# Attention scores as alternating 64-row matmuls in a hybrid attention and mLSTM kernel on one NeuronCore

## The chip, the core and the metric

The kernel runs on one core of one Trainium2 chip. The metric is the device time of one execution in microseconds (us), lower is better. Before the change three runs gave 1333.98, 1334.25 and 1334.64 us; their median, 1334.25 us, is the time before.

## The reference, cut to what matters

Two layers (DEPTH 2) work on 512 tokens of width 1024 in float32. Each layer projects the normalised input once and runs two branches from it: differential attention with 8 heads and an mLSTM with 8 heads. Both are gated, projected back and added. The change is in the attention branch alone. Each head has two maps `r` with their own queries and keys of 64 elements, and one value of 128:

```python
q = rope(rmsnorm(two_map_heads(aq), q_norm_g), cos, sin)   # (1, 8 heads, 512, 2 maps, 64)
k = rope(rmsnorm(two_map_heads(ak), k_norm_g), cos, sin)
...
sc = jnp.einsum('bhqrd,bhkrd->bhrqk', qb, k).astype(jnp.float32) * scale   # qb: a block of 128 queries
p = jax.nn.softmax(jnp.where(causal, sc, -jnp.inf), axis=-1)
a = p[:, :, 0] - lam * p[:, :, 1]
return jnp.einsum('bhqk,bhkd->bhqd', a.astype(v.dtype), v)
```

The sum over `d` in the first einsum runs over 64 elements, half of the 128 rows of TensorE.

## The kernel before, in words

**Precision.** TensorE takes its operands as `float32r` tiles. To keep float32 accuracy every operand is split into a part `hi` that ACT casts and a rest `lo` that DVE subtracts (`split`, line 489), and a product is the sum of three matmuls, hi by hi, hi by lo and lo by hi (`mm3`, line 493).

**Pieces.** A layer is a list of pieces, one for each 128 x 1024 block of weights (`qk0` to `qk3` are the projections of query and key, `av`, `bv` the values, `az`, `ga`, `gb`, `bo`, `bz` the gates, `bqk` the mLSTM's query and key, `woa`, `wob`, `wo` the output projections). `TUNE["order"]` gives their order. Each piece is a run of 128-row matmuls over 512 columns, and between the pieces the steps of the attention heads (`attn_head`, line 1166) and mLSTM heads (`ml_head`) become due at times counted in steps of the pieces (`TUNE["attn"]`, `a0`, `ap`, `ml`, `m0` and so on).

**Order on the engines.** All operations are recorded first (`Recorder.add`, line 165, with a planned cost from `cost`, line 218), then a list scheduler (`schedule`, line 272) simulates five engines and emits one order for each. Its keys are the due times, the costs, a bias for each tile name (`TUNE["bias"]`) and several margins. The order that it emits is fixed in the program; on the chip every engine takes its own list in order and waits for semaphores.

**Scores before.** One piece group `qk c` holds heads 2c and 2c+1. `qk_done` (line 832) takes the tiles and applies norm and rotation; `back` in `qk_back` (line 897) transposes the 128 tokens by 512 features on TensorE into the PSUM tile `qkt` and evicts them to SBUF. There the 64 features of map 0 lie in partitions 0 to 63 and those of map 1 in 64 to 127. The eviction builds for each map a stacked query tile `[hi; lo]` of 128 rows (`qs0`, `qs1`), a key tile `[hi; hi]` (`ks0`, `ks1`), and a key rest `kl0`, `kl1` whose other 64 rows POOL sets to zero (`half_zero`, line 617). For even `c` the first four are parts of a large tile `qk..x`; for odd `c` they are tiles of a pool of 20 slots (`take`, `give`). Then a score needs two matmuls of 128 rows for each map: `[hi; lo]` by `[hi; hi]`, and `[hi; lo]` by `[lo; 0]`. In `qk(j)` (line 1170) `j` counts the four blocks of 128 queries, and n = 128 (j+1) columns of keys are computed, so n is 128, 256, 384 and 512. With two layers, eight heads and four blocks there are 64 such steps of four matmuls each, 256 in all, 64 of each n. The two maps are in two PSUM banks of one tile `sc`.

**Other 8- and 128-row work that the prediction uses.** `gft` and `gct` are transposes of gate rows with only 8 rows in use (four matmuls each, twice in a program); `glf` are transposes with 128 rows and only 8 columns. `msp_a` is the sum over partitions for the norm of an attention head: two matmuls with a matrix of ones (`msh_a`, `msl_a`), or one where a head is in `TUNE["foldA"]` (`ms_front`, line 1276): there DVE adds the two halves first (`fo_a`).

Of the kernel before, what the change touches and what calls it, by code (L numbers as in the profile page):

```python
# [9 lines left out]
F32 = mybir.dt.float32  # L10
# [25 lines left out]

TUNE = {
    "order": (
# [4 lines left out]
    ),  # L43
    "qkt": 5,
    "gct": 15,
    "gls": 6,
    "glf": 5,
    "attn": (1, 5, 5, 8, 9, 13, 15, 16, 19, 24),
    "a0": 23,
    "ap": 18,  # L50
    "a4": 7,
    "ml": (1, 9, 11, 12, 13, 28),
    "ahead": 3,
    "lc": 7,
    "slack": 4956.0,
    "margin": 72.0,
    "pemargin": 206.2,
    "wait": 333.1,
    "swpen": 141896579.9,
    "smargin": 51.6,  # L60
    "pwait": 0.7,
    "wdiff": 3673.3,
    "wsp": 4,
    "kact": (0, 2),
    "qsq": (1, 3),
    "foldA": (2, 3, 5),
# [4 lines left out]
    "prods": 'P1 P5 P2 P6 P3 P7 P4',  # L71
    "acl": 14,
    "gateA": 9,
    "gateM": 4,
    "actp": (0, 2, 3),
    "m0": 217,
    "mp": 15,
    "m4": 9,
    "slots": 20,
    "bias": {'av': 30400.0, 'msp_a': -4350.0, 'wl': 2200.0, 'wo': -3700.0, 'woh': -4650.0, 'ht': 29250.0, 'taz': -4050.0, 'ga': 25150.0, 'gt': -8800.0, 'p': -900.0, 'wo1_P': 27550.0, 'out_0_dram': -5850.0, 'p5_wo': -4950.0, 'rot': 12400.0, 'dq': -4400.0, 'oa': 450.0, 'dd': 31000.0, 'num': 20100.0, 'ld': -7300.0, 'ws1_wo': -2200.0, 'gw': -1100.0, 'hl': -600.0, 'sc': -1500.0, 'uz': -3750.0, 'mk': 7950.0, 'sbz': 4200.0, 'az': 12900.0, 'posi': 3200.0, 'msl_d': 1650.0, 's1_wo': 5000.0, 'msh_d': 6450.0, 'sq': -1400.0, 'warm': 3150.0, 'bo': -450.0, 'sdl': 150.0, 'ml': 16100.0, 'fo_b': 12850.0, 'ws0_wo': -900.0, 'wt1_wo': 1400.0, 'pb': 8800.0, 'sbo': 5350.0, 'qkt': 3900.0, 'junk': 7400.0, 'ulZ': 6400.0, 'bv': 650.0, 'bqk': -1750.0, 'uh': -3950.0, 'ms_b': -1100.0, 'ob': -400.0, 'uy': 1500.0, 'ms': 11100.0, 'ms_a': 1750.0, 'ones': 4150.0, 'msh_b': 8300.0, 'x1d': -3000.0, 'saz': 1000.0, 'xr': -3950.0, 'wo0_P': 450.0, 'qk1_0x': 2050.0, 'msh_a': 6050.0, 'rnh': -3150.0, 'gft': 6600.0, 'gct': 3100.0, 'kl': -700.0, 'qk1_2x': -800.0, 'gf': 1550.0, 'qk0_0x': -1600.0, 'qy': 7250.0, 'msl_a': 1400.0, 'x': -4550.0, 'eps': -600.0, 'wt0_wo': -2500.0, 'xn': 400.0, 'msl_b': 2150.0, 'rn': -400.0, 'glf': -3500.0, 'ss': 7600.0, 'sinv': 6150.0, 'ulA': -2650.0, 'epsc': -3000.0, 'ulB': 950.0, 'ulY': -300.0, 'tbz': 350.0, 'hh': 3700.0, 'fo_a': 6500.0, 'mx': -1800.0, 'gc': -150.0, 'mq': -1050.0, 'ang': 3150.0, 'qt': -2500.0, 'uhZ': -1250.0, 'em': -6800.0, 'ct': 1000.0, 'fo_d': 3850.0, 'par': -250.0, 'ks': 250.0, 'den': -400.0, 'sdh': -1000.0, 'cv': -300.0, 'ng': 3750.0, 'uhB': 300.0, 'rows': -300.0, 'zw': 50.0, 'qs': 1350.0, 'ctab': 950.0, 'gcol': 3400.0, 'ul': 1000.0, 'fb_b': 400.0, 'sums': 400.0, 'cosv': 250.0},  # L80
    "drain": 467.1,
    "risk": 268.4,
    "late": 912.7,
}


# [16 lines left out]
class Recorder:  # L103
# [113 lines left out]
    @staticmethod  # L217
    def cost(eng, fn, a, k):
        def cols(ap):
            n = 1  # L220
            for x in list(ap.shape)[1:]:
                n *= x
            return n

        def ps(ap):
            return isinstance(ap, bass.AP) and ap.space == PSUM

        n = cols(a[0])
        if eng == "PE" and a[0].tensor.name.startswith("warm"):
            return 350.0  # L230
        if eng == "PE":
            n = cols(a[2]) if fn == "matmul" else cols(a[0])
            return max(n / 2.4 + 13.4, 107.5)
        if eng == "POOL":
            return 1000.0 if fn == "dma_start" else 200.0 + n
        if eng == "ACT":
            x = 52 + n * 0.833 + (0 if ps(a[1]) else 42)
            for v in (k.get("bias"), k.get("scale")):
                if isinstance(v, bass.AP):
                    x += 93  # L240
            if k.get("accum_out") is not None:
                x += 93
            return x
        if eng == "DVE":
            aps = [v for v in a[1:] if isinstance(v, bass.AP)]
            if fn == "reciprocal":
                return 64 + 6.26 * n
            if fn == "memset":
                return 8 + n * 1.04
            if fn == "tensor_reduce":  # L250
                return 69 + cols(a[1]) / 0.96
            if fn == "tensor_tensor_scan":
# [192 lines left out]
def kernel(ctx, tc, x, pos, wp, wg, cst, par, pb, ngb, out):  # L445
# [180 lines left out]
    def layer_events(l):  # L626
# [204 lines left out]

        def qk_done(c, tt, acc):
            if tt == 0:
                names = ("qs0", "qs1", "ks0", "ks1")
                if c % 2 == 0:
                    until(lambda: c == 0 or st.get(("A", 1), 0) > 5)
                    xt = big.tile([P, 8, S], F32R, tag="big", name=f"qk{l}_{c}x")
                    st[("qs", c)] = [xt[:, 2 * i : 2 * i + 2, :] for i in range(4)]
                    take(2)
                else:  # L840
                    take(6)
                    st[("qs", c)] = [q2(f"{n}{l}_{c}") for n in names]
                st[("kl", c)] = [half_zero(f"kl{r}{l}_{c}", r) for r in range(2)]
                st[("rq", c)] = cp.tile([P, NT, 8], F32, tag=f"rq{c % 2}", name=f"rq{l}_{c}")
            sq = t2(f"sq{l}_{c}_{tt}")
            if tt % 2 == 0:
# [41 lines left out]
        def qk_back(c, tt, rq):  # L888
            k3 = rq[:, 256:512].rearrange("p (g d) -> p g d", d=64)
            rk = st[("rq", c)][:, tt, 4:8].unsqueeze(2).to_broadcast([P, 4, 64])  # L890
            if tt in TUNE["kact"]:
                for g in range(4):
                    A.activation(k3[:, g, :], k3[:, g, :], AF.Copy, scale=st[("rq", c)][:, tt, 4 + g : 5 + g])
            else:
                V.tensor_tensor(k3, k3, rk, ALU.mult)

            def back():
                pst = ps_tr.tile([P, 4, P], F32, tag="tr", name=f"qkt{l}_{c}_{tt}")
                for g in range(4):
# [12 lines left out]

            defer(TUNE["qkt"], back)
# [252 lines left out]
        def attn_head(h, t0):  # L1166
# [3 lines left out]
            def qk(j):  # L1170
                n = P * (j + 1)
                sc = ps_sc.tile([P, 2, S], F32, tag="sc", name=f"sc{l}_{h}_{j}")
                qs = slice(j * P, (j + 1) * P)
                q, k, kl = st[("qs", c)][0:2], st[("qs", c)][2:4], st[("kl", c)]

                for r in range(2):
                    T.matmul(sc[:, r, :n], q[r][:, hl, qs], k[r][:, hl, :n], start=True, stop=False)
                    T.matmul(sc[:, r, :n], q[r][:, hl, qs], kl[r][:, hl, :n], start=False, stop=True)
                if j == 3 and hl:
                    give(2 if c % 2 == 0 else 6)  # L1180
                dg = sc[:, :, n - P : n]
                V.tensor_tensor(dg, dg, mask_a.unsqueeze(1).to_broadcast([P, 2, P]), ALU.add)
                mx = small(2, f"mx{l}_{h}_{j}")
# [462 lines left out]
```

## Time and profile before

| what | value |
|---|---|
| median of three runs | 1334.25 us (1333.98 to 1334.64) |
| profiled execution, first to last instruction (span) | 1333.4 us |
| granted TensorE clock | 0.999 |
| PE / PEld busy | 99% / 82%, 6200 instructions each |
| DVE / ACT / POOL busy | 76% / 68% / 3% |

The page gives no other time of the profiled execution than its span; the median of the runs lies 0.85 us above it. PE is TensorE's matmul queue and PEld its weight loads (LDWEIGHTS), of which every matmul has one. A matmul's printed duration runs from its start to its modelled end and overlaps its successor, so what a matmul costs in a stream is read from the distance between starts: in the stream of 512-column matmuls that is 0.23 us, though each is printed with 0.39. Rows of a timeline read: start, time taken by the row, engine, line, operation, out<-in, rows*columns of the array in use, shape, and how many were merged.

### The profile page before, as it was taken

How to read it: one execution, taken by the hardware profiler on the slowest of the kernel's cores; microseconds unless marked ns; L12 is line 12 of the kernel's file. 1: busy time of each engine (PE TensorE's matmuls, PEld its weight loads, DVE VectorE, ACT ScalarE, POOL GpSimd, SP SyncE). 2: the span in 40 equal slices, each digit the busy share in tenths (PEclk: the TensorE clock that was granted, in tenths of full speed). 3: DMA queues.
4: the chain of work that ended last, by engine and by line, in shares of the span. 5: the costliest groups of instructions: out<-in, count | busy, mean ns of one | idle time of the engine just before them, and what ended most of it. 6: DMA issues, size and time to landing. Idle time of an engine off the chain costs nothing.

```text
span 1333.4 us, 17564 instructions
## 1 busy us (share of the span) xinstructions
PE 1326.1 (99%) x6200; PEld 1096.4 (82%) x6200; DVE 1018.1 (76%) x1846; ACT 907.4 (68%) x1836; POOL 37.0 (3%) x44
## 2 busy tenths in 40 slices
PE   8999999999999999999999999999999999999998
PEld 7888888888888888888888888888888888888887
DVE  7898899786259967755888988997852698687466
ACT  5878888877237958743667787888762478687243
POOL 1000000000000000000200000000000000000000
PEclk9999999999999999999999999999999999999999
DMA  5222222323344433544832121223232444345546
GB/s 188 87 65 79 80 80 64 95 79 94 100 121 124 119 114 109 154 148 123 258 125 88 49 96 54 89 67 92 82 110 81 123 134 124 98 129 148 170 123 181
DMA packets 51274, 148.15 MB, mean 111 GB/s; under 512 B 6097, under 2 KB 12881, under 8 KB 51185
## 3 DMA queue, kind: packets, MB, share of 16 engines
q1 hardware_dynamic: 48880, 138.63, 33.5%
q0 software_dynamic: 2304, 8.39, 3.5%
q8 instruction: 49, 0.80, 0.3%
q14 instruction: 41, 0.33, 0.1%
HBM read 142.74 MB, written 4.26 MB: 110 GB/s over the span
## 4 chain that ended last, share of the span: by engine, by line
PE 97%; ACT 1%; DVE 1%; DMA 0%; issue 0%; SPq 0%; DVEq 0%
PE qk L441 13%; PE av L441 9%; PE az L441 7%; PE bv L441 7%; PE bo L441 7%; PE bqk L441 7%; PE ga L441 7%; PE woa L441 7%; PE wob L441 7%; PE gb L441 6%; PE bz L441 6%; PE wo_P L441 6%; PE sc L441 3%; PE num L441 2%; PE ut L441 1%; PE ms L441 1%
## 5 line engine op out<-in xcount | busy, mean ns | idle before, releaser
L441 ACT CAST wh<-wr 128x1024 fp32r<-128x1024 f32 (+1 forms) x206 | 214.6, 1044 | 181.9 <-PE wob L441 41.0
L441 DVE TENSOR_TENSOR wl<-wr,wh 128x1024 fp32r<-128x1024 f32 (+1 forms) x208 | 249.0, 1200 | 107.1 <-ACT wh L441 106.3
L441 PE MATMUL qk<-wh,hh 128*128 128x512 f32 x256 | 96.8, 403 | 1.0 <-ACT hh L441 1.0
L441 PE MATMUL qk<-wl,hh 128*128 128x512 f32 x256 | 94.9, 397 | 0.5 <-DVE wl L441 0.5
L441 PE MATMUL qk<-wh,hl 128*128 128x512 f32 x256 | 94.9, 401 | 0.1
L441 ACT ACTIVATE p<-sc,mx,rq 128x128 f32<-128x128 f32 (+3 forms) x128 | 78.9, 619 | 18.5 <-DVE mx L441 17.8
L441 PE MATMUL woa<-oa,wh 128*128 128x512 f32 x256 | 86.4, 389 | 0.0
L441 PE MATMUL wob<-ob,wh 128*128 128x512 f32 x256 | 84.4, 389 | 0.0
L440 ACT ACT_TABLE_LOAD x65 | 83.4, 1283 | 1.1
L441 PEld LDWEIGHTS qk<-wh,hh 128*128 128x128 f32 x256 | 47.8, 189 | 11.1 <-ACT hh L441 1.3
L441 PEld LDWEIGHTS qk<-wl,hh 128*128 128x128 f32 x256 | 48.3, 189 | 9.9 <-DVE wl L441 0.9
L441 PEld LDWEIGHTS wob<-ob,wh 128*128 128x128 f32 x256 | 48.1, 188 | 10.1
L441 PEld LDWEIGHTS qk<-wh,hl 128*128 128x128 f32 x256 | 48.0, 189 | 9.9 <-DVE hl L441 0.4
L441 PEld LDWEIGHTS woa<-oa,wh 128*128 128x128 f32 x256 | 47.9, 188 | 9.9
L441 DVE TENSOR_REDUCE mx<-sc 128x2 f32<-128x256 f32 (+1 forms) x64 | 52.5, 820 | 1.1
L441 PE MATMUL bo<-hh,wl 128*128 128x512 f32 x128 | 50.3, 393 | 0.0
L441 PE MATMUL bo<-hh,wh 128*128 128x512 f32 x128 | 50.2, 392 | 0.0
L441 PE MATMUL bo<-hl,wh 128*128 128x512 f32 x128 | 50.2, 392 | 0.0
L441 PE MATMUL bqk<-hh,wl 128*128 128x512 f32 x128 | 50.0, 393 | 0.0
L441 PE MATMUL bz<-hh,wl 128*128 128x512 f32 x128 | 49.9, 393 | 0.0
L441 PE MATMUL bz<-hl,wh 128*128 128x512 f32 x128 | 49.9, 393 | 0.0
L441 PE MATMUL bz<-hh,wh 128*128 128x512 f32 x128 | 49.9, 392 | 0.0
(309 smaller groups left out, 3692.9 us busy)
## 6 DMA issues: line engine op xcount, KB each, us to landing
wr<-in_wp_dram SPq DMA_DIRECT2D x204, 512.0 KB, 3.6
ws_wo<-in_wp_dram POOLq DMA_DIRECT2D x12, 512.0 KB, 6.7
dd<-rows SPq DMA_DIRECT2D x16, 256.0 KB, 4.0
em<-rows SPq DMA_DIRECT2D x16, 256.0 KB, 3.9
dd<-rows SPq DMA_DIRECT2D x16, 192.0 KB, 5.0
x<-in_x_dram SPq DMA_DIRECT2D x4, 512.0 KB, 7.9
dd<-rows SPq DMA_DIRECT2D x16, 128.0 KB, 6.1
ws_wo<-in_wp_dram SPq DMA_DIRECT2D x4, 512.0 KB, 5.2
```

The costliest lines, as they stand in the source:

```text
L440: self.tc.keep_in_program_order(self.nc.scalar.preload_act_table_set(self.SET_NAME[o["load"]]))
L441: self.tc.keep_in_program_order(getattr(o["e"], o["fn"])(*o["a"], **o["k"]))
```

## The change

The three products of a score are computed separately with 64 rows each. Query and key now have one `hi` and one `lo` tile that hold both maps, map 0 in partitions 0 to 63 and map 1 in 64 to 127, as the transposed `qkt` has them. For each product the matmul of map 0 and that of map 1 follow each other in the program (`R` is the half of the partitions), so that a step has six 64-row matmuls in three pairs in place of four 128-row ones. The eviction becomes a plain `split`. The zero-filled tiles `kl` go, and odd `c` takes four slots where it took six, even `c` none where it took two.

```diff
         if eng == "PE" and a[0].tensor.name.startswith("warm"):
             return 350.0
+        if eng == "PE" and fn == "matmul" and a[1].shape[0] == 64:
+            return max(cols(a[2]) / 4.8 + 7, 107.5)
...
-                names = ("qs0", "qs1", "ks0", "ks1")
+                names = ("qh", "kh", "qlo", "klo")
...
-                    take(2)
+                    st[("qx", c)] = [(xt[:, 0:4, :], xt[:, 4:8, :], slice(0, 4))]
                 else:
-                    take(6)
-                    st[("qs", c)] = [q2(f"{n}{l}_{c}") for n in names]
-                st[("kl", c)] = [half_zero(f"kl{r}{l}_{c}", r) for r in range(2)]
+                    take(4)
+                    qs = st[("qs", c)] = [q2(f"{n}{l}_{c}") for n in names]
+                    st[("qx", c)] = [(qs[0], qs[2], slice(0, 2)), (qs[1], qs[3], slice(2, 4))]
...
-                for q, k, kl, a, b in ((q0, k0, kl0, L, H), (q1, k1, kl1, H, L)):
-                    A.copy(q[a], pst[a, 0:2, :])
-                    V.tensor_tensor(q[b], pst[a, 0:2, :], q[a].bitcast(F32), ALU.subtract)
-                    A.copy(k[a], pst[a, 2:4, :])
-                    A.copy(k[b], pst[a, 2:4, :])
-                    V.tensor_tensor(kl[a], pst[a, 2:4, :], k[a].bitcast(F32), ALU.subtract)
+                for hi, lo, g in st[("qx", c)]:
+                    split(hi[:, :, ts], lo[:, :, ts], pst[:, g, :])
...
-                for r in range(2):
-                    T.matmul(sc[:, r, :n], q[r][:, hl, qs], k[r][:, hl, :n], start=True, stop=False)
-                    T.matmul(sc[:, r, :n], q[r][:, hl, qs], kl[r][:, hl, :n], start=False, stop=True)
-                if j == 3 and hl:
-                    give(2 if c % 2 == 0 else 6)
+                for i, (a, b) in enumerate(((qh, kh), (qh, kl), (ql, kh))):
+                    for r in range(2):
+                        R = slice(64 * r, 64 * r + 64)
+                        T.matmul(sc[:, r, :n], a[R, hl, qs], b[R, hl, :n], start=i == 0, stop=i == 2)
+                if j == 3 and hl and c % 2:
+                    give(4)
```

The planner's cost of a 64-row matmul is about half that of a 128-row one of the same columns, but not less than 107.5 ns. The scheduler's numbers are set anew with it: the order of the pieces, nearly all biases, the due times and the margins. Of these numbers:

```diff
-    "pemargin": 206.2,
-    "wait": 333.1,
+    "pemargin": 0.0,
+    "wait": 182.9,
...
-    "foldA": (2, 3, 5),
+    "foldA": (1, 2, 3, 5, 6, 7),
...
-    "gateM": 4,
-    "actp": (0, 2, 3),
+    "gateM": 2,
+    "actp": (2, 3),
```

So six heads of eight have the single `msp_a` matmul where three had it, and one of the four scalings of `p` (that of 128 columns) goes from ACT to DVE.

The first place is a score step on TensorE in the first layer, head 2, second block of queries (`sc_2_1`; the matmuls `av_1_...` around it are the projection of the second half of the values). Before:

```order
L441 MATMUL av_1_2_333<-wh_301,hl_115 128x512
L441 MATMUL sc_2_1_335<-ks_1_277,qs_1_275 128x256
L441 MATMUL sc_2_1_335<-ks_1_278,qs_1_276 128x256
L441 MATMUL sc_2_1_335<-kl_1_279,qs_1_275 128x256
L441 MATMUL sc_2_1_335<-kl_1_280,qs_1_276 128x256
L441 MATMUL av_1_2_333<-wh_301,hh_114 128x512
```

With the change:

```order
L442 MATMUL av_1_3_312<-wh_271,hl_115 128x512
L442 MATMUL sc_2_1_328<-kh_1_274,qh_1_273 128x256 x2
L442 MATMUL sc_2_1_328<-klo_1_276,qh_1_273 128x256 x2
L442 MATMUL sc_2_1_328<-kh_1_274,qlo_1_275 128x256 x2
L442 MATMUL av_1_3_312<-wh_271,hh_114 128x512
```

Four 128-row matmuls have become six 64-row ones in one stretch (x2 is map 0 and map 1), with 128-row matmuls ahead of and behind them.

The second place is on TensorE too, the same block of head 6 in the first layer, where the step is split. Here `av_5` is the product of head 5's probabilities with the values, and `ut_6_0` a transpose of probabilities. Before, one of the four stood ahead of the `av_5` matmuls and three behind them:

```order
L441 MATMUL av_5_568<-ul_5_532,av_1_0_364 128x512
L441 MATMUL ut_6_0_586<-ct,p_6_0_574 128x128
L441 MATMUL sc_6_1_580<-kl_3_492,qs_3_488 128x256
L441 MATMUL sc_6_1_580<-ks_3_491,qs_3_489 128x256
L441 MATMUL sc_6_1_580<-kl_3_493,qs_3_489 128x256
L441 MATMUL ga_2_579<-hh_114,wl_560 128x512
```

With the change the beginning of the step is

```order
L442 MATMUL az_5_551<-hh_114,wh_539 128x512
L442 MATMUL az_5_551<-hl_115,wh_539 128x512
L442 MATMUL sc_6_1_568<-kh_3_485,qh_3_484 128x256 x2
L442 MATMUL sc_6_1_568<-klo_3_487,qh_3_484 128x256
L442 MATMUL av_5_560<-uh_5_519,av_1_0_348 128x512 x2
```

and its end, twelve rows later,

```order
L442 MATMUL av_5_560<-ul_5_520,av_1_0_348 128x512
L442 MATMUL ut_6_0_574<-ct,p_6_0_566 128x128
L442 MATMUL sc_6_1_568<-klo_3_487,qh_3_484 128x256
L442 MATMUL sc_6_1_568<-kh_3_485,qlo_3_486 128x256 x2
L442 MATMUL az_5_551<-hh_114,wl_540 128x512
```

The step's six matmuls stand in two stretches of three, and the second pair is torn apart. Over the whole program the 384 score matmuls stand in 97 such stretches between 128-row work: 35 of six, 19 of four, 31 of two, and 12 of one, three or five. Before, 256 matmuls stood in 94 stretches, all of 128 rows like their neighbours.

More of the change, by code (lines that the diff above doesn't have):

```diff
@@ L45 @@
     "gct": 15,
-    "gls": 6,
-    "glf": 5,
-    "attn": (1, 5, 5, 8, 9, 13, 15, 16, 19, 24),
+    "gls": 4,
+    "glf": 4,
+    "attn": (1, 5, 5, 8, 10, 14, 16, 17, 20, 25),
     "a0": 23,
     "ap": 18,
-    "a4": 7,
-    "ml": (1, 9, 11, 12, 13, 28),
+    "a4": 3,
+    "ml": (0, 1, 6, 7, 8, 23),
     "ahead": 3,
-    "lc": 7,
-    "slack": 4956.0,
-    "margin": 72.0,
-    "pemargin": 206.2,
-    "wait": 333.1,
+    "lc": 11,
+    "slack": 32.8,
+    "margin": 0.0,
+    "pemargin": 0.0,
+    "wait": 182.9,
     "swpen": 141896579.9,
-    "smargin": 51.6,
-    "pwait": 0.7,
-    "wdiff": 3673.3,
+    "smargin": 0.0,
+    "pwait": 0.0,
+    "wdiff": 7430.9,
     "wsp": 4,
@@ L73 @@
     "gateA": 9,
-    "gateM": 4,
-    "actp": (0, 2, 3),
+    "gateM": 2,
+    "actp": (2, 3),
     "m0": 217,
-    "mp": 15,
+    "mp": 16,
     "m4": 9,
     "slots": 20,
-    "bias": {'av': 30400.0, 'msp_a': -4350.0, 'wl': 2200.0, 'wo': -3700.0, 'woh': -4650.0, 'ht': 29250.0, 'taz': -4050.0, 'ga': 25150.0, 'gt': -8800.0, 'p': -900.0, 'wo1_P': 27550.0, 'out_0_dram': -5850.0, 'p5_wo': -4950.0, 'rot': 12400.0, 'dq': -4400.0, 'oa': 450.0, 'dd': 31000.0, 'num': 20100.0, 'ld': -7300.0, 'ws1_wo': -2200.0, 'gw': -1100.0, 'hl': -600.0, 'sc': -1500.0, 'uz': -3750.0, 'mk': 7950.0, 'sbz': 4200.0, 'az': 12900.0, 'posi': 3200.0, 'msl_d': 1650.0, 's1_wo': 5000.0, 'msh_d': 6450.0, 'sq': -1400.0, 'warm': 3150.0, 'bo': -450.0, 'sdl': 150.0, 'ml': 16100.0, 'fo_b': 12850.0, 'ws0_wo': -900.0, 'wt1_wo': 1400.0, 'pb': 8800.0, 'sbo': 5350.0, 'qkt': 3900.0, 'junk': 7400.0, 'ulZ': 6400.0, 'bv': 650.0, 'bqk': -1750.0, 'uh': -3950.0, 'ms_b': -1100.0, 'ob': -400.0, 'uy': 1500.0, 'ms': 11100.0, 'ms_a': 1750.0, 'ones': 4150.0, 'msh_b': 8300.0, 'x1d': -3000.0, 'saz': 1000.0, 'xr': -3950.0, 'wo0_P': 450.0, 'qk1_0x': 2050.0, 'msh_a': 6050.0, 'rnh': -3150.0, 'gft': 6600.0, 'gct': 3100.0, 'kl': -700.0, 'qk1_2x': -800.0, 'gf': 1550.0, 'qk0_0x': -1600.0, 'qy': 7250.0, 'msl_a': 1400.0, 'x': -4550.0, 'eps': -600.0, 'wt0_wo': -2500.0, 'xn': 400.0, 'msl_b': 2150.0, 'rn': -400.0, 'glf': -3500.0, 'ss': 7600.0, 'sinv': 6150.0, 'ulA': -2650.0, 'epsc': -3000.0, 'ulB': 950.0, 'ulY': -300.0, 'tbz': 350.0, 'hh': 3700.0, 'fo_a': 6500.0, 'mx': -1800.0, 'gc': -150.0, 'mq': -1050.0, 'ang': 3150.0, 'qt': -2500.0, 'uhZ': -1250.0, 'em': -6800.0, 'ct': 1000.0, 'fo_d': 3850.0, 'par': -250.0, 'ks': 250.0, 'den': -400.0, 'sdh': -1000.0, 'cv': -300.0, 'ng': 3750.0, 'uhB': 300.0, 'rows': -300.0, 'zw': 50.0, 'qs': 1350.0, 'ctab': 950.0, 'gcol': 3400.0, 'ul': 1000.0, 'fb_b': 400.0, 'sums': 400.0, 'cosv': 250.0},
@@ L81 @@
-    "drain": 467.1,
-    "risk": 268.4,
-    "late": 912.7,
+    "bias": {'wo': -3700.0, 'woh': -4650.0, 'msl_d': 1650.0, 'msh_d': 6450.0, 'kl': -700.0, 'qk0_0x': -59900.0, 'ks': 250.0, 'qs': 1350.0, 'sgb': -79540.0, 'uh': -10980.0, 'par': -11940.0, 'ng': -3600.0, 'msp_a': -27780.0, 'ms_b': 29450.0, 'qk': -12100.0, 'dd': 9150.0, 'qss': -2190.0, 'zeroc': 49180.0, 'fb_d': -37390.0, 'bo': -4100.0, 'gcol': 6680.0, 'ua': 23340.0, 'junk': 24170.0, 'ct': -5880.0, 'sq': 57550.0, 'hh': 23950.0, 'stab': -17140.0, 'gi': -5840.0, 'msp_b': 19560.0, 'mq': -15830.0, 'ms_a': -8600.0, 'qlo': 24190.0, 'av': -8040.0, 'sdh': 37620.0, 'posi': 21070.0, 'wo0_P': -450.0, 'rnh': 8840.0, 'rows': 770.0, 'kh': 22720.0, 'rot': 14100.0, 'lneps': -28670.0, 'bv': -26970.0, 'gft': 9700.0, 'hl': -3770.0, 'ul': 17870.0, 'p': 35030.0, 'sinv': 6740.0, 'gt': -19000.0, 'mql': -14520.0, 'az': 16350.0, 'wo1_P': 20580.0, 'zw': -18090.0, 'qt': -12110.0, 'ws0_wo': -7310.0, 'tbz': -130.0, 'taz': -8620.0, 'ss': 21550.0, 'ob': 8910.0, 'sbz': -5090.0, 'bz': 32550.0, 'epsc': 16040.0, 'qk1_0x': -18070.0, 'sums': -19780.0, 'fb_b': -22590.0, 'msl_a': 2990.0, 'wl': -550.0, 'ht': -440.0, 'wt1_wo': 16690.0, 'wt0_wo': -30.0, 'mk': -3300.0, 'glf': -1010.0, 'uhZ': -17500.0, 'ws1_wo': -28480.0, 'ulZ': 8200.0, 'x': -560.0, 'cosv': 8560.0, 'lq': -8590.0, 'oa': 2990.0, 'gc': -10590.0, 'qk0_2x': 12140.0, 'out_0_dram': -3070.0, 'ut': 1960.0, 'qh': 970.0, 'num': -31740.0, 'fo_a': -250.0, 'gb': -24450.0, 'uhY': 4290.0, 'msh_b': -300.0, 'wh': 15480.0, 'rn': 18090.0, 'uhB': -2300.0, 'sc': 4090.0, 'ms': -2090.0, 'gw': 7660.0, 'gct': 5850.0, 'cv': 100.0, 's1_wo': -3310.0, 'p5_wo': -3160.0, 'saz': 6370.0, 'fo_d': 1320.0, 'uhA': -16350.0, 'ones': 2850.0, 'wr': -15690.0, 'ga': -10320.0, 'uz': -8880.0, 'warm': -24190.0, 'qy': 1210.0, 'ld': 10860.0, 'em': 4390.0, 'gf': 9610.0, 'eps': 5300.0, 'sdl': -10130.0, 'woa': 740.0, 'rq': 7220.0, 'ulA': -4020.0, 'fo_b': -20470.0, 'bqk': -8980.0, 'den': -460.0, 'wob': 1060.0, 'xr': -2000.0, 'qkt': 1330.0, 'fb_a': -3640.0, 'pb': 620.0, 'ulY': 11780.0, 'sbo': -1080.0, 'x1d': 40.0, 'ctab': 240.0, 'ulB': 170.0, 'qk1_2x': 400.0, 'gm': 150.0, 'ml': -6260.0, 'uy': -3770.0, 'ang': 560.0, 'msl_b': -160.0, 'mx': 250.0},
@@ L84 @@
+    "drain": 470.6,
+    "risk": 1774.4,
+    "late": 488.2,
 }
@@ L901, in back @@
                 ts = slice(tt * P, (tt + 1) * P)
-                q0, q1, k0, k1 = (t[:, :, ts] for t in st[("qs", c)])
-                kl0, kl1 = (t[:, :, ts] for t in st[("kl", c)])
-                L, H = slice(0, 64), slice(64, 128)
-                for q, k, kl, a, b in ((q0, k0, kl0, L, H), (q1, k1, kl1, H, L)):
-                    A.copy(q[a], pst[a, 0:2, :])
-                    V.tensor_tensor(q[b], pst[a, 0:2, :], q[a].bitcast(F32), ALU.subtract)
-                    A.copy(k[a], pst[a, 2:4, :])
-                    A.copy(k[b], pst[a, 2:4, :])
-                    V.tensor_tensor(kl[a], pst[a, 2:4, :], k[a].bitcast(F32), ALU.subtract)
+                for hi, lo, g in st[("qx", c)]:
+                    split(hi[:, :, ts], lo[:, :, ts], pst[:, g, :])
                 st[("qkn", c)] = tt + 1
@@ L1173, in qk @@
                 qs = slice(j * P, (j + 1) * P)
-                q, k, kl = st[("qs", c)][0:2], st[("qs", c)][2:4], st[("kl", c)]
-                for r in range(2):
-                    T.matmul(sc[:, r, :n], q[r][:, hl, qs], k[r][:, hl, :n], start=True, stop=False)
-                    T.matmul(sc[:, r, :n], q[r][:, hl, qs], kl[r][:, hl, :n], start=False, stop=True)
-                if j == 3 and hl:
-                    give(2 if c % 2 == 0 else 6)
+                qh, kh, ql, kl = st[("qs", c)]
+                for i, (a, b) in enumerate(((qh, kh), (qh, kl), (ql, kh))):
[4 more added lines that the diff above has]
+                    give(4)
                 dg = sc[:, :, n - P : n]
```

7 rows, old and new, of the table TUNE are left out of this document.

## Prediction

> **What bounds the kernel now.** I read the page's busy line first, then the chain that ended last, then the waits of PE.
>
> ```profile
> PE 1326.1 (99%) x6200; PEld 1096.4 (82%) x6200; DVE 1018.1 (76%) x1846; ACT 907.4 (68%) x1836; POOL 37.0 (3%) x44
> ...
> PE 97%; ACT 1%; DVE 1%; DMA 0%; issue 0%; SPq 0%; DVEq 0%
> ...
> PE warm L441 <- DVE ml L441: 1.6, 1, 1.6
> PE qk L441 <- ACT hh L441: 1.0, 1, 1.0
> PE qk L441 <- DVE wl L441: 0.5, 1, 0.5
> PE ht L441 <- DVE junk L441: 0.3, 1, 0.3
> ```
>
> PE is the bound: it is 97% of the chain, and the four waits are all that it waits for other engines, 3.4 us in total, on tiles that belong to the start. The scores are made in two stretches, which the view of windows shows (columns: stretch, its length, busy time of PE, PEld, DVE, ACT, POOL, then clock and DMA):
>
> ```profile
> 20.00:300.00 280.00, 280.00 (x1365) 231.23 (x1364) 249.25 (x571) 227.19 (x599) 5.70 (x6) 1.00 0.26 80
> 680.00:960.00 280.00, 280.00 (x1363) 230.91 (x1362) 243.07 (x542) 224.66 (x595) 4.75 (x5) 1.00 0.26 79
> ```
>
> PE has no gap there, and the clock is granted in full. So the time follows the sum of what PE's instructions cost, and nothing else has to be moved to move it.
>
> **What leaves PE, and what the scores cost now.** For each n the timeline of PE has a clean step of four score matmuls between 512-column matmuls. The step's cost runs from its first start to the start of the matmul behind it.
>
> ```profile
> 75.43 0.33 PE L441 MATMUL sc<-qk_0x 128*128 128x128 f32 x2
> 75.60 0.39 PE L441 MATMUL sc<-kl,qk_0x 128*128 128x128 f32 x2
> 75.83 0.45 PE L441 MATMUL qk<-wh,hl 128*128 128x512 f32 x1
> ...
> 56.65 0.40 PE L441 MATMUL sc<-qk_0x 128*128 128x256 f32 x2
> 56.88 0.40 PE L441 MATMUL sc<-kl,qk_0x 128*128 128x256 f32 x2
> 57.12 0.40 PE L441 MATMUL av<-wh,hl 128*128 128x512 f32 x1
> ...
> 63.53 0.51 PE L441 MATMUL sc<-qk_0x 128*128 128x384 f32 x2
> 63.88 0.52 PE L441 MATMUL sc<-kl,qk_0x 128*128 128x384 f32 x2
> 64.24 0.40 PE L441 MATMUL av<-wl,hh 128*128 128x512 f32 x1
> ...
> 136.09 0.62 PE L441 MATMUL sc<-ks,qs 128*128 128x512 f32 x2
> 136.54 0.62 PE L441 MATMUL sc<-kl,qs 128*128 128x512 f32 x2
> 137.00 0.39 PE L441 MATMUL av<-wl,hh 128*128 128x512 f32 x1
> ```
>
> That is 0.40, 0.47, 0.71 and 0.91 us, 2.49 us for the four blocks of a head, and 39.8 us for 16 heads. A step will be three pairs of 64-row matmuls. The trace has no two matmuls on separate halves of the array, so a pair's price has bounds only. If the two run side by side, a pair costs one slot of today: 3/4 of 39.8 is 29.9, a gain of 10.0. If they run one after the other, 6/4 is 59.8, a loss of 19.9. Between them lies a third case, in which the matmuls overlap but each weight load takes its turn (its price is worked out with the rivals, a loss of 2.9). I take the gain of 10.0: the halves share no row, and the two maps write different PSUM banks. It is the least certain choice here.
>
> The Trainium skill ("TensorE: Matmul & The Clock Gate", the section on packing small matmuls) says that matmuls in distinct row groups run concurrently, and measured 3.07 times the speed for four of 32 rows. Scaled to two halves I estimate from that figure a pair at 1.1 slots, by which the gain of 10.0 would be 7; no run here shows it.
>
> Six more `msp_a` matmuls go, one for each of three heads in two layers:
>
> ```profile
> L441 PE MATMUL msp_a<-msh_a,ones x10: 397/398/416, 89.9 to 976.7; 128*128 128x512 f32 x10
> L441 PE MATMUL msp_a<-fo_a,ones x6: 395/400/473, 155.9 to 922.8; 128*128 128x512 f32 x6
> ```
>
> After it the order has 4, 4 and 12 of the three kinds, 20 where 26 stood. At the 0.23 us between 512-column starts (137.00 less 136.54, halved) that is a gain of 1.4.
>
> **What is added: the way into and out of half-height work.** Before, every score matmul used 128 rows as its neighbours did. The trace holds matmuls with fewer rows in four places, `gft` and `gct` with 8 rows. Two of them follow, PE first, then PEld for the first of them, then the loads' durations (least, median and most, in ns):
>
> ```profile
> 131.26 0.39 PE L441 MATMUL av<-wh,hl 128*128 128x512 f32 x1
> 131.58 0.41 PE L441 MATMUL gct<-ct,gi 8*128 8x8 f32 x4
> 131.92 0.50 PE L441 MATMUL av<-wh,hh 128*128 128x512 f32 x1
> 132.26 0.40 PE L441 MATMUL av<-wl,hh 128*128 128x512 f32 x1
> ...
> 790.11 0.40 PE L441 MATMUL av<-wh,hl 128*128 128x512 f32 x1
> 790.44 0.41 PE L441 MATMUL gct<-ct,gi 8*128 8x8 f32 x4
> 790.77 0.50 PE L441 MATMUL av<-wh,hh 128*128 128x512 f32 x1
> 791.11 0.39 PE L441 MATMUL av<-wl,hh 128*128 128x512 f32 x1
> ...
> 131.58 0.32 PEld L441 LDWEIGHTS gct<-ct,gi 8*128 8x128 f32 x4 [0.36 <-issue]
> 131.92 0.19 PEld L441 LDWEIGHTS av<-wh,hh 128*128 128x128 f32 x1
> 132.03 0.19 PEld L441 LDWEIGHTS av<-wl,hh 128*128 128x128 f32 x1
> ...
> L441 PEld LDWEIGHTS gct<-ct,gi x8: 132/136/137, 131.6 to 790.6; 8*128 8x128 f32 x8
> ```
>
> Elsewhere a weight load starts while the matmul ahead of it runs. Here the load of `gct` starts only with its own matmul at 131.58, 0.32 after the last 128-row matmul where 0.23 is usual: 0.09 lost. On the way out the load of `av` again starts with its own matmul. The four `gct` loads take 0.32 with 0.136 for one of them, so they follow each other every 0.06 and the fourth starts at 131.76; the next one at 131.92 comes 0.16 later, 0.10 lost. And the `av` matmul behind it lasts 0.34 to the next start instead of 0.23: 0.11 lost, the load that nothing covers. Together 0.30 us for one visit, and the second visit has the same starts to 0.01 us.
>
> A visit of 64-row score matmuls should pay the same, and up to 0.11 more: its first load is of the kind that takes 0.11 (131.92 to 132.03), and was cheaper with `gct`. So 0.30 to 0.41 for a visit; I take 0.35, and down to 0.24 for the range, in case a short step hides one load that costs it time today. From below, a visit may cost nothing (next part). The order of the change has 97 stretches of score matmuls between 128-row work, and each is one visit: 97 by 0.35 is a loss of 34.0.
>
> The Trainium skill ("TensorEngine Tiling (Array Packing)", the section on tiling modes) says that changing the tiling mode, not just the tile, drains TensorE. By that rule a visit has a price, which the `gct` rows agree with; without the rule the sum below would lose its largest term.
>
> **What costs nothing.** The eviction of `qkt` loses 192 casts on ACT and 128 subtractions on DVE of 64 x 256:
>
> ```profile
> L441 ACT CAST ks<-qkt x64: 364/368/372, 108.3 to 899.0; 64x256 fp32r<-64x256 f32 x64
> L441 DVE TENSOR_TENSOR kl<-qkt,ks x32: 405/422/429, 109.2 to 899.9; 64x256 fp32r<-64x256 f32 x32
> ```
>
> That is 70.7 us of ACT and 54.0 of DVE; 32 operations of 128 x 256 and 16 of 128 x 512 on each engine take their place, at most two of the old durations for the long ones, 24 and 27 us. The rest is relief for engines that work under PE (280 of 280 us busy), as are POOL's zero fills and the freed slots, so I cost them at nothing. They could only remove waits of PE, of which there are 3.4 us, at the start. The scheduler's margins go to nearly zero, so an ACT or DVE operand may now come just too late, and everything on PE queues behind that matmul. PE runs some 30 us behind such a plan by the term above, which gives the others time; I take 0, within -2 and +4.
>
> **Sum.** 1333.4 - 1.4 - 10.0 + 34.0 = 1356.0 us of span. The runs stand 0.85 above the span (1334.25 to 1333.4), so 1356.9, say 1357.
>
> **Rivals.** *A visit is free* (faster). Fewer rows alone need not stop the loads: `glf` uses 8 columns, and PE's rows and the row of its loads are there
>
> ```profile
> 87.40 0.39 PE L441 MATMUL qk<-wl,hh 128*128 128x512 f32 x1
> 87.63 0.60 PE L441 MATMUL glf<-ct,gw 128*8 128x128 f32 x4
> ...
> 87.40 0.53 PEld L441 LDWEIGHTS glf<-ct,gw 128*8 128x8 f32 x4
> ```
>
> with its first load at 87.40 beside the matmul ahead and its first matmul 0.23 later: no price. That is a change of columns and not of rows, and whatever delays `gct` may belong to 8 rows alone. Then 1334.25 - 1.4 - 10.0 = 1323. The point from which this decides is a visit of 11.4/97 = 0.12 us; above it the change loses. Against it stand four places with rows cut, all late on both sides. Chance 0.16.
>
> *Loads one after another.* Consecutive loads start 0.11 apart (131.92, 132.03). If the two halves cannot load together, a pair costs at least 0.22, whatever n: 3 x (0.22 + 0.22 + 0.22 + 0.23) = 2.67 for a head, 42.7 for all, +2.9 where I have -10.0. With visits at 0.35 that is 1370; from 0.30 to 0.41 it is 1365 to 1376. Chance 0.24. With free visits it is 1336, chance 0.07.
>
> *The change doesn't do what it says:* the alternating matmuls don't overlap. Then +19.9, and with visits 1387. Chance 0.05: the 12 odd stretches tear few pairs apart.
>
> *A small price* of 0.10 to 0.15 a visit: 1322.9 + 9.7 to 14.6, 1333 to 1337, with the scheduler's uncertainty around it. Chance 0.05.
>
> **How the numbers follow.** My forecast has 0.43: pairs side by side, visits from 0.24 to 0.41, 1346 to 1363, likeliest 1357. With the serial loads at 0.24 the range must reach 1376; at the low end it takes in the small price and the free visits with serial loads, and 4 us of the scheduler's uncertainty below those, to 1328. It leaves out most of 0.16 and the 0.05. This kernel's runs differ by 0.05%, and 0.2% (2.7 us) is about what a measurement can tell from no change. Faster by more: the free visits and 0.02 of the small price, which the scheduler's uncertainty carries there, 0.18. Within: the serial loads with free visits and 0.02 of the small price, 0.09. Slower: the rest, 0.73.
>
> **What would show it.** In the profile after, at each stretch of `sc`, PEld's first load should start with its matmul and about 0.32 after the last 128-row start, and the 512-column matmul behind the stretch should last 0.34 to the next. Inside a stretch two starts a few hundredths apart and pairs 0.23 apart at n = 512 say side by side; pairs 0.22 apart at n = 128 say serial loads. PE's waits should stay near 3 us. If loads of 64 rows start beside the matmul ahead, the large term is wrong and the kernel is faster; if PE waits for DVE or ACT in 20 to 300 us, the scheduler's part is.

## The result and the profile after

The changed kernel takes 1370.74 us (median of four runs, 1367.35 to 1372.17), the kernel before beside it 1334.45 us: a ratio of 1.0269, 95% interval 1.0255 to 1.0284. It is 36.3 us slower. The two profiled executions have spans of 1369.7 and 1333.4 us, 36.3 us apart as well, so the traces hold the whole difference. (The later runs list both numbers for each execution: a run stands 1.7 to 2.2 us above its own span.)

The page's busy line and chain, and all that PE waits for, of the changed kernel:

```profile
PE 1355.4 (99%) x6322; PEld 1085.3 (79%) x6322; DVE 991.0 (72%) x1788; ACT 849.6 (62%) x1678; POOL 21.8 (2%) x28
...
PE 94%; DMA 3%; DVE 2%; SPq 1%; ACT 0%; issue 0%; DVEq 0%; ACTq 0%
...
PE av L442 <- DVE ul L442: 5.9, 3, 2.9
PE warm L442 <- DVE ml L442: 1.6, 1, 1.6
PE ht L442 <- DVE junk L442: 1.1, 2, 0.8
PE ms L442 <- DVE dd L442: 0.8, 2, 0.4
PE qk L442 <- ACT hh L442: 0.7, 1, 0.7
PE qk L442 <- DVE wl L442: 0.3, 1, 0.3
```

ACT and DVE have become lighter by 58 and 27 us and that bought nothing: PE is still the bound. Two things are new. PE now waits 10.4 us where it waited 3.4, most of it for `ul` of attention head 7, and a DMA stands in the chain. And PE itself has more to do. The step of scores that the order showed, first on PE, then on PEld:

```profile
120.11 0.39 PE L442 MATMUL av<-wh,hl 128*128 128x512 f32 x1
120.43 0.38 PE L442 MATMUL sc<-kh,qh 64*128 64x256 f32 x2
120.66 0.28 PE L442 MATMUL sc<-klo,qh 64*128 64x256 f32 x2
120.77 0.28 PE L442 MATMUL sc<-kh,qlo 64*128 64x256 f32 x2
120.98 0.50 PE L442 MATMUL av<-wh,hh 128*128 128x512 f32 x1
121.32 0.60 PE L442 MATMUL qkt<-ct,rot 128*128 128x128 f32 x4
...
120.43 0.19 PEld L442 LDWEIGHTS sc<-kh,qh 64*128 64x128 f32 x2 [0.35 <-ACT kh L442]
120.54 0.19 PEld L442 LDWEIGHTS sc<-klo,qh 64*128 64x128 f32 x2
120.66 0.19 PEld L442 LDWEIGHTS sc<-kh,qlo 64*128 64x128 f32 x2
120.98 0.19 PEld L442 LDWEIGHTS av<-wh,hh 128*128 128x128 f32 x1
```

Three things are to be read here. Two matmuls of a pair take 0.28 us together, as long as one, and the pairs follow each other by 0.11 (120.66 to 120.77), the slot of one 128-row matmul of 256 columns. The two loads of a pair run side by side too (x2 in 0.19), pair after pair 0.11 apart. And the way in and out has its price: the first load starts with its own matmul, 0.32 behind the last 128-row start, and the second pair starts 0.23 behind the first where 0.11 is usual; the load of `av` again starts with its matmul at 120.98, and that matmul is 0.34 from the next.

To see how much this is in all, I summed starts over the trace: a stretch of scores costs what lies between the start of the matmul ahead of it and that of the second one behind it, less the ordinary slot of every matmul in it that isn't a score (0.2273 us at 512 columns, at least 0.108). With all else sorted in the same way the difference of the spans closes (5.4 us ahead of the first matmul and behind the last are the same in both):

| part of PE's time, us | before | after | difference |
|---|---|---|---|
| score stretches (94 and 97) | 41.4 | 68.4 | +27.0 |
| ordinary slots of all other matmuls | 1269.0 | 1267.7 | -1.3 |
| lost beyond the slots after the first 20 us | 11.1 | 22.8 | +11.7 |
| the same in the first 20 us | 6.4 | 5.4 | -1.0 |

So 27 us belong to the 64-row matmuls, and 12 us to places where PE stood or ran slowly. The two largest of those are alike, one in each layer. The first, on PE, then on DVE, then the load in the chain that ended last (start, us), then the window behind it (its columns as in the prediction's first windows):

```profile
323.07 0.34 PE L442 MATMUL av<-uh,av 128*128 128x256 f32 x2
326.06 0.48 PE L442 MATMUL av<-ul,av 128*128 128x128 f32 x1 [2.65 <-DVE ul L442]
...
321.77 0.55 DVE L442 TENSOR_TENSOR ul<-ut,uh 128x384 fp32r<-128x384 f32 x1
325.37 0.43 DVE L442 TENSOR_TENSOR dd<-dd,ct 128x256 f32<-128x256 f32 x1 [3.05 <-DMA dd<-rows]
325.72 0.28 DVE L442 TENSOR_TENSOR ul<-ut,uh 128x128 fp32r<-128x128 f32 x1
...
317.28 8.00 DMA dd<-rows
...
327.00:332.00 5.00, 5.00 (x13) 3.86 (x12) 3.14 (x4) 3.42 (x5) 0.00 (x0) 0.50 0.11 15
```

In DVE's list the mask addition on `dd`, the decay table of the first mLSTM head, stands ahead of the last `ul` of attention head 7. It waits 3.05 us for its load, `ul` waits behind it, and PE waits 2.65 us for `ul`. And in the 5 us of the window the granted clock is 0.50: a 512-column matmul takes 0.427 us where it takes 0.227. In whole the half clock lasts from 325.6 to 332.4. The same happens in the second layer, with a wait of 2.92 us and half the clock from 1004.8 to 1008.3. Outside the first 20 us PE's waits sum to 6.7 us, and the matmuls at half speed add 4.7 (3.6 of it in the 18 matmuls of 512 columns that ran at it from start to end); the two are 11.4 of the 11.7.

### The profile page after: what moved, and what is told of

Read it like the earlier page. It is cut to its first block, busy times and chain, and to the rows that moved or that the text cites. A ratio compares the mean times of both kernels' runs of the same rounds, so it can differ in the third digit from the quotient of the medians.

```text
span 1369.7 us, 17564 instructions
## 1 busy us (share of the span) xinstructions
PE 1355.4 (99%) x6322; PEld 1085.3 (79%) x6322; DVE 991.0 (72%) x1788; ACT 849.6 (62%) x1678; POOL 21.8 (2%) x28
## 4 chain that ended last, share of the span: by engine, by line
PE 94%; DMA 3%; DVE 2%; SPq 1%; ACT 0%; issue 0%; DVEq 0%; ACTq 0%
PE qk L442 13%; PE av L442 9%; PE az L442 7%; PE bv L442 7%; PE ga L442 7%; PE gb L442 6%; PE wob L442 6%; PE bz L442 6%; PE woa L442 6%; PE bqk L442 6%; PE bo L442 6%; PE wo_P L442 6%; PE sc L442 4%; DMA dd<-rows 2%; PE num L442 2%; PE ut L442 1%
## 5 line engine op out<-in xcount | busy, mean ns | idle before, releaser
L442 PE MATMUL qk<-wh,hh 128*128 128x512 f32 x256 | 93.1, 401 | 0.7 <-ACT hh L442 0.7
L442 PE MATMUL woa<-oa,wh 128*128 128x512 f32 x256 | 89.8, 402 | 0.0
L442 PE MATMUL wob<-ob,wh 128*128 128x512 f32 x256 | 81.2, 389 | 0.0
L442 PEld LDWEIGHTS wob<-ob,wh 128*128 128x128 f32 x256 | 48.0, 188 | 10.2 <-DVE ob L442 0.3
L442 PE MATMUL az<-hh,wl 128*128 128x512 f32 x128 | 51.9, 406 | 0.0
L442 PE MATMUL az<-hl,wh 128*128 128x512 f32 x128 | 51.7, 404 | 0.0
L442 DVE TENSOR_TENSOR ul<-ut,uh 128x128 fp32r<-128x128 f32 (+2 forms) x80 | 33.5, 419 | 24.3 <-ACT uh L442 18.1
L442 PE MATMUL az<-hh,wh 128*128 128x512 f32 x128 | 50.9, 398 | 0.0
L442 PE MATMUL av<-wl,hh 128*128 128x512 f32 x128 | 50.4, 409 | 0.0
```

Source lines behind the costliest of these rows:

```text
L442: self.tc.keep_in_program_order(getattr(o["e"], o["fn"])(*o["a"], **o["k"]))
```

## The experiments

All timed against the kernel before on the same chip, whose median was 1333.7 to 1334.2 us. In what was written before the runs, theory V is that a visit to 64-row work costs about 0.4 us and that the pairs run side by side.

**The plan and the code, crossed (e1, e2).** The whole table `TUNE` of one kernel in the other: e1 is the code of before with the changed kernel's table, e2 the changed code with the table of before. In e2, for one of its entries:

```diff
-    "pemargin": 0.0,
+    "pemargin": 206.2,
...
```

> The kernel before, with 128-row score matmuls, under all scheduler numbers of the changed kernel (folds included). Theory V (each stretch of 64-row matmuls costs about 0.4 us to enter and leave, and the waits at head 7 come from the new plan): six matmuls fewer, -1.4, plus at most the two waits of PE on ul and the half clock behind them, up to 9: 1333 to 1342 us. Rival P (the new plan is what costs): 1355 us or more.

> The changed score code under all scheduler numbers of the kernel before. The plan puts the score matmuls into 134 stretches, and the mask addition on dd behind the last ul on DVE. Theory V: 1334.3 - 10 + 134 x 0.41 = 1379 us, and no wait of PE for ul of more than 1 us. Rival P: within 10 us of the kernel before, 1334 to 1344.

e2 gave 1377.80 us (ratio 1.0330, 1.0315 to 1.0346), as theory V had it: PE's waits sum to 3.3 us, the same as before the change, and 134 stretches cost 85.1 us by the method above. So the score code alone loses more than 40 us under a plan that makes PE wait for nothing more. And what is lost beyond the slots after the first 20 us is about 11 us in e2, as in the kernel before (11.1): the 11.7 us more of the changed kernel come with its new scheduler numbers, and the old numbers do without them.

e1 missed theory V: 1396.34 us (1.0476, 1.0458 to 1.0493), 26 us slower than the changed kernel. Taken by its time alone it is what rival P said. Its profile shows that it is another trouble:

```profile
PE msp_a L440 <- DVE fo_a L440: 12.1, 4, 3.4
PE ut L440 <- DVE ul L440: 4.5, 2, 2.2
PE qk L440 <- DVE av L440: 3.9, 2, 2.0
PE av L440 <- DVE sq L440: 3.6, 2, 1.8
```

PE's waits sum to 41 us, where the changed kernel has 10.4. The scheduler makes a new order from the same numbers for other operations, and this order is bad on the chip. What follows is that the new numbers can't be carried over to the old code, and that the effect of the code has to be read from the stretches and not from the time of e1.

**The late mask (e3).** The planner's landing time of the loads from `rows`:

```diff
-                end[i] = max(dma, go) + 2000.0
+                end[i] = max(dma, go) + (9000.0 if <source is rows> else 2000.0)
```

> The changed kernel, with the planner told that the loads dd from rows land 9 us after issue instead of 2: on DVE the mask additions on dd then stand behind the last ul of head 7; the 97 stretches on TensorE stay. Theory V with the late load as a second cause: the two waits of PE of 2.65 and about 3.0 us, the shorter ones beside them and the half-speed matmuls behind them go, 7 to 10 us less: 1361 to 1364 us. Rival (PE waits there for something else, or the wait comes back a little later): within 2 us of the changed kernel, about 1370.

It was slower, 1375.77 us (1.0316, 1.0301 to 1.0332), with the score stretches unchanged at 68.4 us. The wait for `ul` is gone, and the mask additions stand far behind, at 334.39 and 335.54. But now `fo_a`, the fold of head 7, is late: on DVE a weight piece `wl` stands ahead of it, which waits for ACT, and ACT for the piece's load. First ACT, then DVE:

```profile
326.38 1.05 ACT L442 CAST wh<-wr 128x1024 fp32r<-128x1024 f32 x1 [4.58 <-DMA wr<-in_wp_dram]
...
327.46 1.23 DVE L442 TENSOR_TENSOR wl<-wr,wh 128x1024 fp32r<-128x1024 f32 x1 [5.33 <-ACT wh L442]
328.61 0.68 DVE L442 TENSOR_TENSOR ms_a<-ms_a,fb_a 64x512 f32<-64x512 f32 x1
329.97 0.69 DVE L442 TENSOR_TENSOR fo_a<-ms_a,fo_a 64x512 fp32r<-64x512 f32 x1 [0.68 <-ACT fo_a L442]
```

PE waits 6.0 us for `fo_a` in the two layers, and 4.2 for operands of `wob` at the end of each layer. The rival holds: the wait came back a little later, with another owner.

**Fewer stretches (e4).** The scheduler prefers a 64-row matmul right after a 64-row matmul, and the first of a step waits for what the others wait for.

```diff
+                for o in rec.ops[first + 1 :]:
+                    for w, v in o["pre"].items():
+                        if w < first:
+                            rec.ops[first]["pre"].setdefault(w, v)
...
+                    if e == "PE" and half and self.half(ops[i]):
+                        k -= 1e9
```

> The changed kernel, with the scheduler held to issue the six score matmuls of a step in a row: 70 stretches instead of 97, the same 384 matmuls. Theory V: 27 visits less at 0.41, -11 us: about 1360. Rival S (the price is that of 64-row matmuls one by one, such as weight loads that take turns): no change within 2 us, about 1370.

1360.58 us (1.0200, 1.0185 to 1.0215): 10.2 us less for 27 visits less, with the same matmuls. The stretches cost 57.5 us, 10.9 less. Rival S falls.

**More stretches (e6).** The same code with the preference turned round after each pair.

```diff
-                        k -= 1e9
+                        k += -1e9 if half == 1 else 1e9
```

> e4_six_together turned round: the scheduler puts other matmuls between the three pairs of a step, 198 stretches, nearly all of one whole pair. Theory V: 128 visits more than e4 at 0.38 to 0.41, 49 to 52 us more: 1407 to 1413. Rival S (a price by matmul, not by visit): within 3 us of e4.

1408.39 us (1.0561, 1.0545 to 1.0577), 47.8 more than e4 for 128 visits more, 0.37 us each. A pair by itself looks so:

```profile
62.63 0.50 PE L451 MATMUL sc<-qk_0x 64*128 64x512 f32 x2
63.06 0.49 PE L451 MATMUL av<-wh,hl 128*128 128x512 f32 x1
63.48 0.50 PE L451 MATMUL sc<-qk_0x 64*128 64x512 f32 x2
63.91 0.73 PE L451 MATMUL av<-wh,hl 128*128 128x512 f32 x2
64.48 0.38 PE L451 MATMUL ut<-ct,p 128*128 128x128 f32 x2
```

From start to start the `av` matmul between the two pairs takes 0.42, and the pair behind it 0.43; each has a slot of 0.23, so a visit costs 0.39, about half of it on either.

**The order inside a step (e5, e9, e10).** e5 was to compute map 0 first and then map 1; the scheduler put the maps back in turn, so it repeated e4 and gave its time again, 1360.27 us (1.0202, 1.0185 to 1.0219). e9 and e10 fix the order with a dependency of each matmul on the one ahead.

```diff
-                for i, (a, b) in enumerate(((qh, kh), (qh, kl), (ql, kh))):
-                    for r in range(2):
+                for r in range(2):
+                    for i, (a, b) in enumerate(((qh, kh), (qh, kl), (ql, kh))):
...
+                for w in range(first + 1, first + 6):
+                    rec.ops[w]["pre"].setdefault(w - 1, 0)
```

> e4_six_together with the six matmuls of a step in another order: the three products of map 0, then the three of map 1, so that neighbours use the same half of the array. The same 70 stretches. Theory V: only neighbours on different halves run side by side, so a step takes up to six slots where it took three, about 31 us more than e4: 1385 to 1392. Rival (the halves overlap in any order, or not even when they alternate): within 3 us of e4, 1358 to 1364.

> e4_six_together with the order inside a step laid down too, map 0 and map 1 in turn: 64 stretches of exactly six, no torn pair. Theory V: 6 visits and 6 torn pairs less than e4, 2 to 4 us: 1356 to 1359.

> e9 with three products of map 0 and then three of map 1 in each step, laid down as well (in e5 the scheduler had put the maps back in turn, so that e5 was e4 again). The same 64 stretches. Theory V: neighbours on the same half can't run side by side, five slots or six in place of three, 20 to 31 us more than e9: 1377 to 1390. Rival (the halves run side by side in any order): within 3 us of e9.

e9, with 64 whole stretches, took 1355.10 us (1.0162, 1.0143 to 1.0180). e10 took 1354.77 (1.0160, 1.0142 to 1.0179): no difference, against the expectation. In e10 the program has, on TensorE for head 2's first block (the first three use map 0, the last three map 1):

```
L451 MATMUL sc_2_0_319<-kh_1_274,qh_1_273 128x128
L451 MATMUL sc_2_0_319<-klo_1_276,qh_1_273 128x128
L451 MATMUL sc_2_0_319<-kh_1_274,qlo_1_275 128x128
L451 MATMUL sc_2_0_319<-kh_1_274,qh_1_273 128x128
L451 MATMUL sc_2_0_319<-klo_1_276,qh_1_273 128x128
L451 MATMUL sc_2_0_319<-kh_1_274,qlo_1_275 128x128
```

and the chip ran, in the order of starts:

```profile
111.12 0.33 PE L451 MATMUL sc<-kh,qh 64*128 64x128 f32 x2
111.28 0.28 PE L451 MATMUL sc<-klo,qh 64*128 64x128 f32 x2
111.39 0.28 PE L451 MATMUL sc<-kh,qlo 64*128 64x128 f32 x2
111.61 0.50 PE L451 MATMUL az<-hl,wh 128*128 128x512 f32 x1
```

The two `sc<-kh,qh` matmuls are the first of map 0 and the first of map 1, which is fourth in the program; they start 0.01 us apart. Over all heads with tiles of these names the two starts of a pair lie 10 ns apart in the median of e10 and 3 in e4, e5 and e9: the order laid down in e10 did reach the chip, and that of e5 did not. The halves run side by side whether they alternate or not, for three matmuls ahead at least; inside a whole step the alternation in the change's name buys no time.

**The best 64-row kernel that I could make (e7, e11, e12).** e7 is e4 with the planner's margins of the kernel before, e11 is e9 with a landing time of 18 us in place of e3's 9.

```diff
-    "pemargin": 0.0,
+    "pemargin": 206.2,
...
-                end[i] = max(dma, go) + 2000.0
+                end[i] = max(dma, go) + (18000.0 if <source is rows> else 2000.0)
```

> e4_six_together with the planner's slack, margins, waits and penalties of the kernel before; order of pieces, biases and due times stay those of the changed kernel. Again 70 stretches. Theory M (the late operands and the half clock behind them come from planning without margin): PE's waits fall to those at the start, and about 9 us of e4's 1360.6 go: 1350 to 1353; the rest above the kernel before, 16 to 18 us, is the visits' price less the pairs' gain. Rival (the waits come from the new order and due times): within 3 us of e4, 1358 to 1364.

> e9 with the loads dd planned to land 18 us after issue, so that on DVE the mask additions on dd of the first mLSTM head stand behind ul and fo_a of attention head 7 (in e3, with 9 us, they stood ahead of fo_a, and PE waited for that). Theory L (the waits at head 7 and the half clock behind them are the late load held in DVE's queue): PE's waits on ul and fo_a there go, 7 to 10 us less than e9, 1347 to 1351 us; what is left above the kernel before is the visits' price less the pairs' gain. Rival (another operand is late there at once): within 3 us of e9.

Both missed: e7 1369.00 us (1.0268, 1.0252 to 1.0283) with 14.0 us of waits of PE, e11 1387.39 us (1.0403, 1.0385 to 1.0422) with 31.6. Theory M falls: the old margins alone don't make a good order of the new numbers. The expectation of e11 has e3 wrong, as the rows of e3 above show; it is in e9 that a mask addition stands ahead of `fo_a` on DVE, at 318.79, and waits 3.15 us for its load. In e11 it is gone from there, and PE still waits 4.2 us for `fo_a`, behind a weight piece once more. Planning anew can't test theory L, since each of these plans brought waits of its own. So e12 keeps the changed kernel's order word for word and moves only the six operations on `dd` of each layer's first mLSTM head, behind the last operation of head 7.

```diff
         for i in order:
...
-            self.tc.keep_in_program_order(getattr(o["e"], o["fn"])(*o["a"], **o["k"]))
+            if i not in moved:
+                emit(i)
+            for w in behind.get(i, ()):
+                emit(w)
```

> The changed kernel with its plan kept word for word, except that the two mask additions and four exponentials on dd of the first mLSTM head of each layer are issued behind the last operation of attention head 7 (the order of TensorE, of the loads and of all else is the changed kernel's; e3 and e11 had planned the rest anew). Theory L: the two waits of PE on ul, 2.65 and about 3 us, and the half clock behind them, about 3.6 us, go: 1361 to 1364 us. Rival (another operand is late there at once): 1368 to 1372.

1366.38 us (1.0241, 1.0224 to 1.0258), 4.4 less than the changed kernel: about half of what theory L had said, and between its range and the rival's. PE's waits, and DVE and PE where the new one arises:

```profile
PE msp_a L449 <- DVE fo_a L449: 3.0, 2, 1.6
...
327.83 1.22 DVE L449 TENSOR_TENSOR wl<-wr,wh 128x1024 fp32r<-128x1024 f32 x1 [2.15 <-ACT wh L449]
329.08 0.69 DVE L449 TENSOR_TENSOR fo_a<-ms_a,fo_a 64x512 fp32r<-64x512 f32 x1
...
329.91 0.47 PE L449 MATMUL msp_a<-fo_a,ones 128*128 128x512 f32 x1 [1.41 <-DVE fo_a L449]
```

The waits for `ul` are gone, and behind the first 20 us no matmul of this execution runs at half speed any more. But 6 us later PE now reaches the fold of head 7 ahead of DVE, which has a weight piece in front of it that waits for ACT and its load, as in e3. PE's waits are 8.3 us where the changed kernel has 10.4. So the late `dd` load did hold DVE's queue and PE, and moving the six operations gave 4.4 us. Most of that is the clock and not the wait: the one run of the changed kernel at a clock of 1.000 has a span of 1365.3 us, 0.1 to 1.4 above the four of e12 (1363.9 to 1365.2). The rest of the lost time has another owner right behind.

**The old scores with more folds (e8).**

```diff
-    "foldA": (2, 3, 5),
-    "foldM": (0, 1, 2, 3, 4, 7),
+    "foldA": (0, 1, 2, 3, 4, 5, 6, 7),
+    "foldM": (0, 1, 2, 3, 4, 5, 6, 7),
```

> The kernel before with foldA and foldM set to all eight heads: 14 of the 512-column matmuls msp_a and msp_b go, 14 x 0.227 = 3.2 us; DVE and ACT take the folds. If PE does not wait for them: 1331.0, a ratio of 0.9976. If it does: 1334 or more.

1355.67 us (1.0157, 1.0139 to 1.0175): the slots of the other matmuls fell by 3.2 us (1269.0 to 1265.8), and PE's waits rose from 3.4 to 17.4. No kernel here beats the one before.

The stretches of six kernels in one table, with the cost by the method above:

| run | stretches | score stretches, us | above 31.1, each | PE's waits, us |
|---|---|---|---|---|
| before (128 rows) | 94 | 41.4 | | 3.4 |
| e9 | 64 | 54.8 | 0.37 | 9.4 |
| e4 | 70 | 57.5 | 0.38 | 9.9 |
| after | 97 | 68.4 | 0.38 | 10.4 |
| e2 | 134 | 85.1 | 0.40 | 3.3 |
| e6 | 198 | 107.5 | 0.39 | 9.0 |

31.1 is 3/4 of 41.4, three pairs at one slot each. One price of 0.37 to 0.40 us explains every row over a threefold range. The rows e9 and e6 alone, without a word on the pairs, give 0.39 for each stretch more and 29.6 us for none, close to the 31.1. Of the other kernels with 64-row scores e3 and e12 have the 68.4 of the changed kernel, e5 the 57.5 of e4, and e10 and e11 are within 0.5 us of e9; e7 has 65.7 with 70 stretches, because PE waits inside them, 3.4 us for `kh` alone.

## Why the prediction came out as it did

The direction was right; the likeliest time, 1357, was 14 us too low. The measured time lies in the range, 1328 to 1376, but that is luck: the case I believed in ended at 1363, and the range went on to 1376 for the serial loads, which did not come. Of the 14 us, 3 are the scores and 11 the scheduler's numbers. Step by step:

- *What bounds the kernel* was right. The relief of ACT and DVE bought no time.
- *Pairs side by side*, the choice that I called the least certain, was right: 0.11 us from pair to pair at 256 columns, where one 128-row matmul had 0.12.
- *The visit* was right in kind and a little small: 0.35 taken, 0.24 to 0.41 as bounds, 0.38 measured. The 0.30 us of `gct` did not hold the load of 0.11 us in full, as the text said. With 97 stretches this gave +27.0 for pairs and visits together where the sum had +24.0. The Trainium skill ("TensorEngine Tiling (Array Packing)", tiling modes) says that a change of tiling mode drains TensorE; the trace agrees for rows, with 0.38 us for way in and out together. Fewer columns alone, the 8 of `glf`, had no price in the trace; whether they are a change of mode in the page's sense, no run here shows.
- *The folds* were right: -1.3 measured, -1.4 in the sum.
- *What costs nothing* is where it failed. I took 0, within -2 and +4, for the scheduler's new numbers, with the argument that a PE behind its plan gives the others time. Measured are +11.7, less 1.0 at the start, and e2 shows that they come with those numbers. The argument missed that DVE ran its list in order, as its rows show: being ahead doesn't help DVE when the operation at the head of its list waits for a load that takes 8.0 us to land and was planned at 2. It also missed that both long waits, 2.65 and 2.92 us, were followed by half speed, 4.7 us of the 11.7. The sign that I gave for it, a wait of PE in 20 to 300 us, pointed at the wrong place: there PE is busy for 280.00 of 280 us, and the long waits stand at 326 and 1005. Of the plan's part 4.4 us were shown to be the late mask with the half speed behind it (e12); the rest was only located, as waits of PE at the joints between the attention and mLSTM heads.
- *The rival of serial loads* named the measured time, 1370, with a mechanism that is not there: loads of a pair start together. That its number fits is chance, the sum of a larger visit and the plan's waits.
- *The rival of the free visit* is refuted by e4 and e6. The point at which the change would begin to pay, 0.12 us a visit, is a third of the price.

## What to carry to other kernels

Half-height matmuls pay here only if the work between entering and leaving saves more than 0.38 us: a step of three pairs saves one slot, at most 0.23 us and 0.16 in the mean (10.3 us over 64 steps), so no order with a stretch for each step can win, not even the 64 whole stretches of e9. By these numbers a stretch would need three steps in a row; no run tried that. Count the stretches in the emitted order before you count matmuls. And a change of a planned kernel is a change of the whole plan: what its numbers bring or cost has to be read apart from what the code does, best by keeping the order and moving the few operations in question.

## What the runs showed of the hardware that I had not expected

- Matmuls on different halves of the rows start 0.01 us apart even where the program has three of one half first (e10, 1354.77 us against 1355.10 with the halves in turn). The Trainium skill ("TensorE: Matmul & The Clock Gate", packing small matmuls) says that matmuls in distinct row groups run concurrently, which agrees, and that matmuls are never reordered; by starts, e10 shows the second otherwise for two halves.
- About a wait of PE of 2.65 us the granted clock fell to 0.50 for 6.8 us, though the matmuls around it were dense. The four runs of the changed kernel have spans of 1365.3, 1367.8, 1369.7 and 1370.1 us at mean clocks of 1.000, 0.998, 0.996 and 0.996: the spread of 0.35% fits the 4.7 us of half speed in the profiled one, which has 0.996. So one program meets the half speed in some executions and not in others; whether its waits differed there is not recorded. In e12, where the longest single wait behind the first microseconds is 1.6 us, the mean clock was 0.998 to 1.000 and the spread 0.1%. These runs give no length of wait from which it comes: in e3 a wait of 1.41 us at 592 stands ahead of 3.4 us at 0.50, after two shorter ones (0.48 and 0.23 us) close before it, and in e1 one of 2.87 us at 65 is followed by a clock of 1.00.
